# Pacing the modulation products by weight tiles, a third buffer for their weight, and silu of c by exp and ln

## The chip, the cores and the metric

The kernel runs on one core of a Trainium2 chip. The metric is device time in microseconds (us) for one execution of the whole program, and the median of several executions stands for a kernel. The engines are named as in the profile: PE is TensorE, DVE is VectorE, ACT is ScalarE, POOL is GpSimd, and SP is SyncE, which issues nearly all the DMAs here.

## The reference

Two blocks are chained on 256 tokens of width 1024. The first holds a mixed layer (mLSTM and a sparse attention, "NSA") and an HGRN2 layer. The second is modulated by a vector `c`:

```python
c_act = jax.nn.silu(c)
for i in range(DEPTH):                     # DEPTH = 2
    mod = c_act @ ada_w[i] + ada_b[i]      # (1, 1024) @ (1024, 6144)
    sh1, sc1, g1, sh2, sc2, g2 = jnp.split(mod, 6, axis=-1)
    h = modulate(rmsnorm(x, norm_mix_g[i]), sh1, sc1)
    y = pool_mixer(h, ...) if i == 0 else sgu_mixer(h, ...)
    x = x + g1[:, None, :] * y
    h = modulate(rmsnorm(x, norm_mlp_g[i]), sh2, sc2)
    x = x + g2[:, None, :] * (jnp.square(jax.nn.relu(h @ mlp_w1[i])) @ mlp_w2[i])
return rmsnorm(x, final_g)
```

The modulation needs only `c` and `ada_w`, nothing of `x`. So its 2 x 48 products (128 columns each) may be done anywhere between the arrival of `c` and the first use of their result.

## The kernel before

**Weight tiles.** All large products go through 128x1024 weight pieces. `load_raw` (L142) fetches two pieces, 1 MB, into a buffer `raw` (three of them); `split_w` (L148) makes from each piece a rounded part `whi` on ScalarE (L153) and the rest `wlo` on VectorE (L154), four buffers each. `mm_T` (L207) then does 24 matmuls for a piece: weight high by activation high (L212), weight high by activation low (L213), weight low by activation high (L214). `tiles_tok` does the same with the roles swapped (L197 to L199). Results leave PSUM through VectorE (`nt`, L301).

**Stages in time.** The mixed layer takes 35 pieces of `ev_w_in` and 8 of `ev_w_out`, with the NSA and mLSTM steps (generators `ns` and `ml`) between them; the HGRN layer takes 32 pieces of `od_w_in` and 8 of `od_w_out`; then come the pool mixer, the first MLP (32 pieces of its first matrix, 32 of its second), the SGU mixer and the second MLP. In the profile these start at about 0, 197, 345, 382 (second matrix 478), 570 and 645 us.

**Modulation.** `ada` (L328) is a generator. Each of its 72 steps takes one or two of the 96 tiles: a DMA of 512 KB into a buffer `araw` (L341, two buffers), then one VectorE instruction that multiplies it by silu of c (`row_c`) and sums along the row into a column of `mod` (L342). Eight tiles are six steps. Silu of c is made after the first NSA and mLSTM steps: one tanh on ScalarE (`tanh(th, crow)`, shown at L371, the line of the table helper) and two VectorE instructions (L489, L490); the scratch is an `araw` buffer.

**What sets the order.** Code calls `step(upto)` at hand-chosen places. The tile scheduler then orders every engine's queue by priority and by free buffers; a step stands there with its priority moved (`tc.high_priority(offset=-50)`). The engines execute their queues in order, so a VectorE instruction that waits for its DMA holds up everything behind it, the `wlo` of the next weight piece among it, and SP's DMA issues wait in the same way for a free buffer.

Of the kernel before, what the change touches and what calls it, by code (L numbers as in the profile page):

```python
# [65 lines left out]
def tile_kernel(ctx: ExitStack, tc: tile.TileContext, io: dict, out: bass.AP):  # L66
# [115 lines left out]
    def tile_T(ps, w, i, pair):  # L182

        wh, wl = w.piece(i, 128)
        mm_T(ps, lambda k: wh[:, k, :], lambda k: wl[:, k, :], pair.hi, pair.lo, range(KT))

    def tiles_tok(w, i, pair, evict):

        ps = [gbank()[:, :256] for _ in range(2)]
        for half in range(2):  # L190
            wh, wl = w.piece(i + half, 256)
            for tb in range(2):
                ts_ = slice(tb * 128, tb * 128 + 128)
                for k4 in range(4):
                    k = half * 4 + k4
                    st, sp = k == 0, k == KT - 1
                    PE.matmul(ps[tb], pair.hi(k)[:, ts_], wh[:, k4, :], start=st, stop=False)  # L197
                    PE.matmul(ps[tb], pair.lo(k)[:, ts_], wh[:, k4, :], start=False, stop=False)  # L198
                    PE.matmul(ps[tb], pair.hi(k)[:, ts_], wl[:, k4, :], start=False, stop=sp)  # L199
        for tb in range(2):  # L200
            evict(tb, ps[tb])
# [102 lines left out]
    def out_proj(src, pair, evict, side=0, every=1):  # L304
        w = Weights(lambda c: src[c])
        for n in range(8):
            if every and n % every == 0:
                step(side)
            ps = gbank()[:, :T]
            tile_T(ps, w, n, pair)  # L310
            evict(n, ps)
# [17 lines left out]
    def ada(crow):  # L329
# [5 lines left out]
        for layer in range(2):  # L335
            mod, gains = mods[layer]
            for i in range(6):
                for n in ((0, 1), (2,), (3,), (4, 5), (6,), (7,)):
                    for c in (i * 8 + j for j in n):
                        raw = mk(wpool, [128, 1024], F32, "araw", bufs=2)  # L340
                        nc.sync.dma_start(raw, io["ada_w"][layer, c])  # L341
                        V.tensor_tensor_reduce(raw, raw, crow, 1.0, P("ada_b", layer * 48 + c), ALU.mult, ALU.add, mod[:, c : c + 1])  # L342
# [6 lines left out]
    done = [0]  # L349

    def step(upto):

        if done[0] < 6 * upto:
            done[0] += 1
            with tc.high_priority(offset=-50):
                next(side[0])

    def finish(upto):
        while done[0] < 6 * upto:
            step(upto)  # L360
# [21 lines left out]
    def even_layer(norm, nxt, w):  # L382
        with ExitStack() as es:
# [81 lines left out]
            def run(it, n=1):  # L465
                for _ in range(n):
                    next(it)
                    if early:
                        step(2)
# [3 lines left out]
            early = []  # L473
# [4 lines left out]
            row_sv = bcast_rows(ev, "sv")  # L478
            crow = bcast_rows(base, "c")
            columns(EV_TILES[4:11])  # L480
# [5 lines left out]

            th = mk(wpool, [128, 1024], F32, "araw", bufs=2)
            tanh(th, crow, scale=0.5)
            V.scalar_tensor_tensor(crow, th, 1.0, crow, op0=ALU.add, op1=ALU.mult)  # L489
            V.tensor_scalar(crow, crow, 0.5, None, op0=ALU.mult)  # L490
            side.append(ada(crow))
# [3 lines left out]
            early.append(1)  # L495
# [5 lines left out]
            early.clear()  # L501
# [8 lines left out]
            out_proj(io["ev_w_out"], y, add_x(nxt), 5, 2)  # L510
# [266 lines left out]
    def hgrn_layer(norm, nxt):  # L777
        with ExitStack() as es:
# [30 lines left out]
            def col(part, h, fn):  # L809
                ps = gbank()[:, :T]  # L810
                if part == 3 or h < 4:
                    step(5)
# [20 lines left out]
            def iv_cols(h0):  # L833
                for c0 in (h0 * 128, h0 * 128 + 256):
                    step(5)
# [109 lines left out]
            out_proj(io["od_w_out"], y, add_x(nxt), 5, 1)  # L945
# [46 lines left out]
    def mlp(layer, mod, norm, nxt):  # L992
        with ExitStack() as es:
# [6 lines left out]
            for n in range(32):  # L1000
                if layer == 0 and n % 2 == 0:
                    step(11)
                if layer and n % 4 == 3:
                    step(12)
# [11 lines left out]
            for n in range(8):  # L1016
                ps = gbank()[:, :T]
                for c in range(4):
                    if layer == 0 and c % 2 == 0:
                        step(11)  # L1020
# [31 lines left out]
    def sgu_layer(consts, mod, gains, norm, nxt):  # L1052
        with ExitStack() as es:
# [7 lines left out]
            def gelu_tile(dst, n):  # L1061
                step(11)
# [261 lines left out]
```

## Time and profile before

| | us |
|---|---|
| median of 3 executions | 840.6 |
| lowest, highest | 839.73, 841.76 |
| the profiled execution, its time | 842.29 |
| its span in the trace | 840.5 |
| PE busy in that span | 810.0 |
| DVE busy | 667.1 |
| ACT busy | 516.3 |

The profiled execution is 1.7 us above the median and 1.8 us longer than its own span. A matmul of a dense row of pieces is listed with about 283 ns, but these overlap: 24 of them follow each other within some 2.9 us. A busy PE is therefore told by the gaps that remain, which the profile lists with what ended them. A row of a window gives its start and end, its length, the busy time (and the count of instructions) of PE, PEld (TensorE's weight load), DVE, ACT and POOL, the granted TensorE clock as a share of full speed, the busy share of the DMA engines, and GB/s; a window asked for TensorE alone has its time only.

### The profile page before, as it was taken

How to read it: one execution, taken by the hardware profiler on the slowest of the kernel's cores; microseconds unless marked ns; L12 is line 12 of the kernel's file. 1: busy time of each engine (PE TensorE's matmuls, PEld its weight loads, DVE VectorE, ACT ScalarE, POOL GpSimd, SP SyncE). 2: the span in 40 equal slices, each digit the busy share in tenths (PEclk: the TensorE clock that was granted, in tenths of full speed). 3: DMA queues.
4: the chain of work that ended last, by engine and by line, in shares of the span. 5: the costliest groups of instructions: out<-in, count | busy, mean ns of one | idle time of the engine just before them, and what ended most of it. 6: DMA issues, size and time to landing. Idle time of an engine off the chain costs nothing.

```text
span 840.5 us, 17614 instructions
## 1 busy us (share of the span) xinstructions
PE 810.0 (96%) x7172; PEld 772.0 (92%) x7172; DVE 667.1 (79%) x1247; ACT 516.3 (61%) x918; POOL 4.9 (1%) x19
## 2 busy tenths in 40 slices
PE   6999999998999999999999998999999999999996
PEld 5989787888998998999999998999999999999995
DVE  7679888899999999999998977756678777754542
ACT  6645656686876565658777633445647777754431
POOL 0000000001000000000000000000000000000000
PEclk9999999999999999999999999999999999999998
DMA  9664266657785777667888888865445454554521
GB/s 328 220 221 171 101 198 218 233 180 265 293 310 201 239 254 282 228 226 246 310 277 289 297 298 295 296 208 194 152 151 185 166 198 161 193 188 168 196 102 50
DMA packets 34497, 184.72 MB, mean 220 GB/s; under 512 B 3825, under 2 KB 4465, under 8 KB 19057
## 3 DMA queue, kind: packets, MB, share of 16 engines
q1 hardware_dynamic: 33984, 182.85, 62.3%
q8 instruction: 56, 0.92, 0.4%
q10 hardware_dynamic: 432, 0.76, 0.3%
q14 instruction: 25, 0.20, 0.1%
HBM read 182.55 MB, written 1.05 MB: 218 GB/s over the span
## 4 chain that ended last, share of the span: by engine, by line
PE 66%; DMA 13%; DVE 10%; ACT 5%; issue 4%; SPq 0%; DVEq 0%; ACTq 0%
PE g L212 17%; PE g L214 17%; PE g L213 16%; DMA araw<-in_ada_w_dram 12%; DVE wlo L154 4%; DVE araw L342 3%; ACT whi L153 1%; PE m L848 1%; PE g L197 1%; PE g L198 1%; PE g L199 1%; PE m L739 1%; PE long L767 1%; PE m L285 1%; DVE nt L301 1%
## 5 line engine op out<-in xcount | busy, mean ns | idle before, releaser
L212 PE MATMUL g<-ahi,whi 128*128 128x258 f32 (+1 forms) x1256 | 359.6, 289 | 10.9 <-ACT whi L153 6.7
L214 PE MATMUL g<-ahi,wlo 128*128 128x258 f32 (+1 forms) x1256 | 356.6, 285 | 3.1 <-DVE wlo L154 3.1
L213 PE MATMUL g<-alo,whi 128*128 128x258 f32 (+1 forms) x1256 | 357.7, 286 | 0.1
L153 ACT CAST whi<-raw 128x1024 fp32r<-128x1024 f32 (+1 forms) x238 | 246.6, 1043 | 168.2 <-PE g L213 134.1
L154 DVE TENSOR_TENSOR wlo<-raw,whi 128x1024 fp32r<-128x1024 f32 (+1 forms) x238 | 289.2, 1217 | 73.7 <-ACT whi L153 73.2
L212 PEld LDWEIGHTS g<-ahi,whi 128*128 128x128 f32 x1256 | 238.3, 190 | 15.6 <-ACT whi L153 6.9
L214 PEld LDWEIGHTS g<-ahi,wlo 128*128 128x128 f32 x1256 | 238.9, 190 | 5.3 <-DVE wlo L154 4.3
L213 PEld LDWEIGHTS g<-alo,whi 128*128 128x128 f32 x1256 | 239.5, 191 | 2.6 <-issue 1.2
L214 PE MATMUL g<-ghi,wlo 128*128 128x256 f32 x512 | 144.5, 282 | 4.5 <-DVE wlo L154 4.4
L213 PE MATMUL g<-glo,whi 128*128 128x256 f32 x512 | 144.7, 283 | 0.0
L212 PE MATMUL g<-ghi,whi 128*128 128x256 f32 x512 | 144.7, 283 | 0.0
L342 DVE CUSTOM_DVE_ANT_0 araw<-araw,row_c,prm 128x1024 f32<-128x1024 f32 x96 | 122.6, 1280 | 25.8 <-DMA araw<-in_ada_w_dram 25.6
L214 PEld LDWEIGHTS g<-ghi,wlo 128*128 128x128 f32 x512 | 96.9, 189 | 5.8 <-DVE wlo L154 5.8
L213 PEld LDWEIGHTS g<-glo,whi 128*128 128x128 f32 x512 | 96.4, 188 | 0.1
L212 PEld LDWEIGHTS g<-ghi,whi 128*128 128x128 f32 x512 | 96.0, 187 | 0.0
L301 DVE TENSOR_TENSOR nt<-g,nrstd 128x256 f32<-128x256 f32 x133 | 55.6, 420 | 21.7 <-PE g L214 21.6
L1012 ACT ACTIVATE nt<-nt,nb 128x256 f32<-128x256 f32 x64 | 32.3, 507 | 19.5 <-DVE nb L1011 19.5
L271 ACT ACTIVATE ahi<-xT,gains 128x256 fp32r<-128x256 f32 x32 | 16.2, 506 | 38.7 <-DVE xT L321 38.0
L197 PE MATMUL g<-whi,ahi 128*128 128x256 f32 x112 | 32.7, 292 | 0.0
L198 PE MATMUL g<-whi,alo 128*128 128x256 f32 x112 | 32.0, 286 | 0.0
L199 PE MATMUL g<-wlo,ahi 128*128 128x256 f32 x112 | 32.0, 286 | 0.0
L277 ACT ACTIVATE sq<-xT 128x256 f32<-128x256 f32 x56 | 22.5, 404 | 12.0 <-DVE xT L321 10.9
(288 smaller groups left out, 824.8 us busy)
## 6 DMA issues: line engine op xcount, KB each, us to landing
raw<-in_mlp_w_dram SPq DMA_DIRECT2D x64, 1024.0 KB, 4.9
araw<-in_ada_w_dram SPq DMA_DIRECT2D x96, 512.0 KB, 5.1
raw<-in_ev_w_in_dram SPq DMA_DIRECT2D x17, 1024.0 KB, 5.4
raw<-in_od_w_in_dram SPq DMA_DIRECT2D x16, 1024.0 KB, 5.6
raw<-in_sgu_w_in_dram SPq DMA_DIRECT2D x8, 1024.0 KB, 4.7
raw<-in_ev_w_out_dram SPq DMA_DIRECT2D x4, 1024.0 KB, 4.9
raw<-in_od_w_out_dram SPq DMA_DIRECT2D x4, 1024.0 KB, 6.0
raw<-in_sgu_w_out_dram SPq DMA_DIRECT2D x4, 1024.0 KB, 4.8
```

Of the source, the lines that this page charges most:

```text
L153: S.copy(hi[:, c], r[:, c])
L154: V.tensor_sub(lo[:, c], r[:, c], hi[:, c])
L197: PE.matmul(ps[tb], pair.hi(k)[:, ts_], wh[:, k4, :], start=st, stop=False)
L198: PE.matmul(ps[tb], pair.lo(k)[:, ts_], wh[:, k4, :], start=False, stop=False)
L199: PE.matmul(ps[tb], pair.hi(k)[:, ts_], wl[:, k4, :], start=False, stop=sp)
L212: PE.matmul(ps, wh(k), ah(k), start=st, stop=False)
L213: PE.matmul(ps, wh(k), al(k), start=False, stop=False)
L214: PE.matmul(ps, wl(k), ah(k), start=False, stop=sp)
L277: S.activation(sq, xT[:, k, :], AF.Square)
L301: V.tensor_tensor(t, ps[:, :T], self.r, op=ALU.mult)
L342: V.tensor_tensor_reduce(raw, raw, crow, 1.0, P("ada_b", layer * 48 + c), ALU.mult, ALU.add, mod[:, c : c + 1])
L1012: S.activation(r, r, AF.Relu, bias=b)
```

## The change

- `step` loses its argument and its guard. All calls at hand-chosen places go away (the mixed layer, both output projections, the HGRN columns, both MLPs, the SGU), and the flag `early` with them.
- A counter of multiplied weight takes their place: `pace(8)` in `tile_T` and in the second matrix of an MLP, `pace(16)` in `tiles_tok`. A table `PACE` of (count, steps) pairs says how many steps are to be done by then, linear in between. It asks for 14 steps by the end of `ev_w_in`, 16 by the end of `ev_w_out`, 25 and 30 by the ends of the HGRN layer's two, 36 about the end of the MLP's first matrix, 60 about the end of its second, 66 and 72 after that. The pool mixer's two pieces call no `pace`, while the table leaves room for 16 there, so from the MLP on each point comes two pieces late.
- `araw` gets three buffers instead of two.
- Silu of c is made as `c * exp(-ln(1 + exp(-c)))`, right after `c` is loaded: two VectorE instructions and three ScalarE ones, of functions that the table set loaded there already has. The steps may start at once.

```diff
     def tile_T(ps, w, i, pair):
+        pace(8)
     def tiles_tok(w, i, pair, evict):
+        pace(16)
-    def out_proj(src, pair, evict, side=0, every=1):
+    def out_proj(src, pair, evict):
-            if every and n % every == 0:
-                step(side)
-                        raw = mk(wpool, [128, 1024], F32, "araw", bufs=2)
+                        raw = mk(wpool, [128, 1024], F32, "araw", bufs=3)
-    done = [0]
-    def step(upto):
-        if done[0] < 6 * upto:
-            done[0] += 1
-            with tc.high_priority(offset=-50):
-                next(side[0])
+    done = [0, 0]
+    PACE = ((88, 0), (280, 14), (344, 16), (600, 25), (664, 30), (936, 36), (1192, 60), (1320, 66), (1384, 66), (1640, 72))
+    def step():
+        done[0] += 1
+        with tc.high_priority(offset=-50):
+            next(side[0])
+    def pace(tiles):
+        u = done[1]
+        done[1] += tiles
+        for (u0, s0), (u1, s1) in zip(PACE, PACE[1:]):
+            if u0 <= u < u1:
+                while done[0] * (u1 - u0) < s0 * (u1 - u0) + (s1 - s0) * (u - u0):
+                    step()
             crow = bcast_rows(base, "c")
+            zc = mk(wpool, [128, 1024], F32, "araw", bufs=3)
+            V.tensor_scalar(zc, crow, -80.0, None, op0=ALU.max)
+            tab[0].activation(zc, zc, AF.Exp, scale=-1.0)
+            tab[0].activation(zc, zc, AF.Ln, bias=1.0)
+            tab[0].activation(zc, zc, AF.Exp, scale=-1.0)
+            V.tensor_tensor(crow, crow, zc, op=ALU.mult)
+            side.append(ada(crow))
             tab[0] = Table(EXP_TANH, tab[0])
-            th = mk(wpool, [128, 1024], F32, "araw", bufs=2)
-            tanh(th, crow, scale=0.5)
-            V.scalar_tensor_tensor(crow, th, 1.0, crow, op0=ALU.add, op1=ALU.mult)
-            V.tensor_scalar(crow, crow, 0.5, None, op0=ALU.mult)
-            side.append(ada(crow))
```

What the scheduler makes of it is seen in the queues of the built programs, in three places. In these rows L342 is listed as ISA, a second row without sources goes with it, and a name's number tells its buffer's use.

The first place is ScalarE's queue some 23 us into the program, where the first weight pieces after the norm are split (`whi`) and results go to `nqk`. Before:

```order
L443 ACTIVATE nqk_165<-nt_271,prm_71 128x256
L153 CAST whi_323<-raw_321 128x1024
L443 ACTIVATE nqk_165<-nt_303,prm_71 128x256
L153 CAST whi_355<-raw_321 128x1024
L598 ACTIVATE A_617<-nqk_165 128x512
L153 CAST whi_389<-raw_387 128x1024
```

Now:

```order
L452 ACTIVATE nqk_165<-nt_271,prm_71 128x256
L380 ACTIVATE araw_320<-araw_320 128x1024
L153 CAST whi_329<-raw_327 128x1024
L452 ACTIVATE nqk_165<-nt_303,prm_71 128x256
L380 ACTIVATE araw_320<-araw_320 128x1024
L153 CAST whi_361<-raw_327 128x1024
L380 ACTIVATE araw_320<-araw_320 128x1024
L153 CAST whi_395<-raw_393 128x1024
```

The three activations of silu (L380) stand one ahead of each of three casts.

The second place is VectorE's queue in the mixed layer, at about 86 us: the first block of the NSA softmax (`nsmc`, `nEc`, `nmx`), the mLSTM's convolution (`qk`) and the weight split (`wlo`). Before:

```order
L722 TENSOR_REDUCE nsmc_934<-nEc_942 128x8
L154 TENSOR_TENSOR wlo_1113<-raw_1110,whi_1112 128x1024
L723 RECIPROCAL nsmc_934<-nsmc_934 128x8
L420 SCALAR_TENSOR_TENSOR qk_161<-mqk_1024,prm_71,qk_161 128x256
L724 TENSOR_TENSOR nsmc_934<-nsmc_934,gtok_693 128x4x2
L420 SCALAR_TENSOR_TENSOR qk_161<-mqk_1064,prm_71,qk_161 128x256
L725 TENSOR_TENSOR nEc_942<-nEc_942,nsmc_934 128x8x15
```

Now:

```order
L154 TENSOR_TENSOR wlo_1058<-raw_1055,whi_1057 128x1024
L728 TENSOR_REDUCE nsmc_948<-nEc_956 128x8
L429 SCALAR_TENSOR_TENSOR qk_161<-mqk_1044,prm_71,qk_161 128x256
L729 RECIPROCAL nsmc_948<-nsmc_948 128x8
L429 SCALAR_TENSOR_TENSOR qk_161<-mqk_1044,prm_71,qk_161 128x256
L730 TENSOR_TENSOR nsmc_948<-nsmc_948,gtok_699 128x4x2
L342 ISA araw_1008,mod_9_88<-araw_1008,row_c_318,prm_71 128x1024
L342 ISA mod_9_88 128x1
L731 TENSOR_TENSOR nEc_956<-nEc_956,nsmc_948 128x8x15
L429 SCALAR_TENSOR_TENSOR qk_161<-mqk_1044,prm_71,qk_161 128x256
L342 ISA araw_1011,mod_9_88<-araw_1011,row_c_318,prm_71 128x1024
```

The weight split has moved ahead of the softmax's sum, and modulation tiles stand between the softmax's instructions where there were none.

The third place is SP's queue of DMA issues in the second matrix of the first MLP, from its fourth fetch on; `raw` is 1 MB of the matrix, `araw` 512 KB of modulation weight. Before:

```order
L144 DMA raw_972_6313<-in_mlp_w2_dram 128x2048
L341 DMA araw_1049_6976<-in_ada_w_dram 128x1024
L144 DMA raw_979_6376<-in_mlp_w2_dram 128x2048
L341 DMA araw_1058_7046<-in_ada_w_dram 128x1024
L341 DMA araw_1059_7049<-in_ada_w_dram 128x1024
L144 DMA raw_986_6440<-in_mlp_w2_dram 128x2048
L341 DMA araw_1065_7110<-in_ada_w_dram 128x1024
```

Now:

```order
L144 DMA raw_957_6269<-in_mlp_w2_dram 128x2048
L341 DMA araw_1414_9317<-in_ada_w_dram 128x1024
L144 DMA raw_966_6338<-in_mlp_w2_dram 128x2048
L144 DMA raw_972_6399<-in_mlp_w2_dram 128x2048
L144 DMA raw_981_6468<-in_mlp_w2_dram 128x2048
```

The last modulation DMA stands ahead of the fifth of sixteen fetches; eleven fetches follow each other alone. Before, modulation DMAs went on up to the fifteenth.

## Rows read from the trace of the kernel before

**Rows 1.** The page: engines' busy time; the chain that ended last, by engine.

```profile
PE 810.0 (96%) x7172; PEld 772.0 (92%) x7172; DVE 667.1 (79%) x1247; ACT 516.3 (61%) x918; POOL 4.9 (1%) x19
...
PE 66%; DMA 13%; DVE 10%; ACT 5%; issue 4%; SPq 0%; DVEq 0%; ACTq 0%
```

**Rows 2.** Windows by stage: length, busy us (count) by engine, clock, DMA.

```profile
20.00:84.00 64.00, 61.85 (x523) 56.76 (x523) 49.85 (x98) 36.42 (x54) 0.53 (x1) 1.00 0.58 208
84.00:136.00 52.00, 49.97 (x340) 41.95 (x339) 44.01 (x108) 34.04 (x95) 0.60 (x6) 0.97 0.51 173
136.00:197.00 61.00, 58.56 (x418) 48.78 (x416) 55.77 (x130) 40.88 (x102) 0.00 (x0) 1.00 0.61 207
197.00:243.00 46.00, 44.89 (x423) 43.82 (x424) 43.38 (x77) 36.11 (x60) 2.71 (x2) 1.00 0.81 290
243.00:300.00 57.00, 54.73 (x1137) 51.93 (x1136) 55.66 (x101) 36.01 (x60) 0.00 (x0) 1.00 0.66 227
300.00:370.00 70.00, 69.86 (x532) 65.30 (x531) 65.78 (x121) 41.49 (x74) 0.00 (x0) 1.00 0.73 259
370.00:478.00 108.00, 107.96 (x874) 106.26 (x874) 101.92 (x209) 80.41 (x149) 0.00 (x0) 1.00 0.80 277
478.00:570.00 92.00, 87.47 (x715) 85.96 (x714) 66.04 (x90) 36.62 (x46) 0.00 (x0) 1.00 0.81 279
```

**Rows 3.** Waits by engine and line: us in total, times, longest.

```profile
PE g L214 <- DVE wlo L154: 7.5, 8, 2.4
DVE araw L342 <- DMA araw<-in_ada_w_dram: 25.6, 25, 2.4
```

**Rows 4.** The modulation instruction, ns min/median/max; its DMA to landing, us.

```profile
L342 DVE CUSTOM_DVE_ANT_0 araw<-araw,row_c,prm x96: 1233/1280/1291, 106.2 to 544.1; 128x1024 f32<-128x1024 f32 x96
...
DMA to landing us min/median/max: 3.4/5.1/9.2
```

**Rows 5.** VectorE's waits for modulation weight: 197:243, 243:300, 300:370, 370:478 us.

```profile
DVE araw L342 <- DMA araw<-in_ada_w_dram: 1.3, 2, 0.9
...
DVE araw L342 <- DMA araw<-in_ada_w_dram: 1.3, 2, 0.8
...
DVE araw L342 <- DMA araw<-in_ada_w_dram: 1.6, 2, 0.8
...
DVE araw L342 <- DMA araw<-in_ada_w_dram: 4.9, 6, 1.5
```

**Rows 6.** Timeline (start, us, instruction, [idle before]): ScalarE at 74 us, TensorE at 25.

```profile
74.15 1.05 ACT L371 ACTIVATE araw<-row_c 128x1024 f32<-128x1024 f32 x1
...
24.99 0.39 PE L212 MATMUL g<-ahi,whi 128*128 128x256 f32 x1 [0.26 <-ACT whi L153]
```

**Rows 7.** Timeline of VectorE, 78 to 82 us: the silu of c.

```profile
78.30 1.21 DVE L489 SCALAR_TENSOR_TENSOR row_c<-araw,row_c 128x1024 f32<-128x1024 f32 x1
...
81.49 0.67 DVE L490 TENSOR_SCALAR row_c<-row_c 128x1024 f32<-128x1024 f32 x1
```

**Rows 8.** TensorE near 88 us: timeline, and a window with its clock.

```profile
88.29 0.58 PE L214 MATMUL g<-ahi,wlo 128*128 128x256 f32 x1 [1.26 <-DVE wlo L154]
...
86.00:92.00 6.00, 4.74 (x25) 0.72 0.02 4
```

**Rows 9.** The chain of waits within 84 to 197 us, by line.

```profile
by line: PE g L214 11.3%; PE g L212 10.5%; PE g L213 10.3%; PE m L739 9.5%; PE long L767 9.4%; PE m L760 6.2%; ACT A L744 3.0%; ACT whi L153 2.9%; PE long L768 2.4%; issue 2.3%; PE m L569 2.2%; DVE wlo L154 2.0%; PE m L579 1.8%; PE m L548 1
```

**Rows 10.** Timeline of TensorE in the chunk levels of the HGRN layer.

```profile
249.76 0.76 PE L848 MATMUL m<-hq,hk 128*32 128x32 f32 x64 [0.89 <-DVE hk L897]
...
254.91 0.75 PE L848 MATMUL m<-hq,hk 128*32 128x32 f32 x64 [1.35 <-DVE hk L897]
```

**Rows 11.** Second matrix of the first MLP: VectorE, TensorE, a window.

```profile
506.11 1.28 DVE L342 CUSTOM_DVE_ANT_0 araw<-araw,row_c,prm 128x1024 f32<-128x1024 f32 x1 [2.35 <-DMA araw<-in_ada_w_dram]
...
508.60 0.39 PE L214 MATMUL g<-ghi,wlo 128*128 128x256 f32 x1 [2.37 <-DVE wlo L154]
...
485.00:490.00 5.00, 4.42 (x37) 4.21 (x37) 4.16 (x7) 1.29 (x3) 0.00 (x0) 1.00 0.94 337
```

More of the change, by code (lines that the diff above doesn't have):

```diff
@@ L348, in tile_kernel @@
     side = []
-    done = [0]
-    def step(upto):
-        if done[0] < 6 * upto:
-            done[0] += 1
-            with tc.high_priority(offset=-50):
-                next(side[0])
+    done = [0, 0]
[4 more added lines that the diff above has]
+            next(side[0])
     def finish(upto):
         while done[0] < 6 * upto:
-            step(upto)
+            step()
[5 more added lines that the diff above has]
+                while done[0] * (u1 - u0) < s0 * (u1 - u0) + (s1 - s0) * (u - u0):
+                    step()
     class Table:
@@ L467, in run @@
                     next(it)
-                    if early:
-                        step(2)
             nout = mk(ev, [128, 4, T], F32, "nout")
             mout = mk(ev, [128, 4, T], F32, "num")
-            early = []
             columns(EV_TILES[:4])
@@ L494, in even_layer @@
             columns(EV_TILES[17:23])
-            early.append(1)
             run(ns)
@@ L500, in even_layer @@
                 run(ns, n)
-            early.clear()
             columns(EV_TILES[25:31])
@@ L509, in even_layer @@
             columns(EV_TILES[31:])
-            out_proj(io["ev_w_out"], y, add_x(nxt), 5, 2)
+            out_proj(io["ev_w_out"], y, add_x(nxt))
     def mlstm(ev, et, qk, v, gsb, num, tanh):
@@ L810, in col @@
                 ps = gbank()[:, :T]
-                if part == 3 or h < 4:
-                    step(5)
                 tile_T(ps, w, part * 8 + h, pair)
@@ L834, in iv_cols @@
                 for c0 in (h0 * 128, h0 * 128 + 256):
-                    step(5)
                     tiles_tok(w, 8 + c0 // 128, pair, lambda tb, ps: V.scalar_tensor_tensor(
@@ L944, in hgrn_layer @@
             finish(2)
-            out_proj(io["od_w_out"], y, add_x(nxt), 5, 1)
+            out_proj(io["od_w_out"], y, add_x(nxt))
     def pool_layer(band, mod, norm, nxt):
@@ L1000, in mlp @@
             for n in range(32):
[L1001 to L1004, printed above, removed]
                 if layer == 0 and n == 16:
@@ L1018, in mlp @@
                 for c in range(4):
-                    if layer == 0 and c % 2 == 0:
-                        step(11)
+                    pace(8)
                     wh, wl = w2.piece(4 * n + c, 128)
@@ L1061, in gelu_tile @@
             def gelu_tile(dst, n):
-                step(11)
                 ps = gbank()[:, : norm.pair.w]
```

## The prediction

> **What bounds the kernel now.** I read the page first. TensorE is busy 96% of the span, and the chain that ended last is two thirds TensorE and 13% DMA [rows 1]: a change can win only where TensorE still has a gap, and lose only where it opens one. Next I read the windows by stage [rows 2]; length minus TensorE's busy time is the gap. From 20 to 84 us it is 2.2 us, 84 to 136 us 2.0, 136 to 197 us 2.4, 197 to 243 us 1.1, 243 to 300 us 2.3, 300 to 370 us 0.1, 370 to 478 us nothing, and 478 to 570 us, the first MLP's second matrix, 4.5. The same rows show VectorE's load: 44.0 of 52 us and 55.8 of 61 us in the mixed layer, over 94% from 197 to 370 us and in the MLP's first matrix, but only 66.0 of 92 us in its second. So the largest gap is where VectorE has least to do. The waits tell why [rows 3]: TensorE waits for `wlo`, while VectorE waits 25 times and 25.6 us for modulation weight. One case [rows 11]: VectorE stands 2.35 us for `araw`, then does the tile, then the `wlo` for which TensorE has stood 2.37 us. A modulation tile takes 1.28 us, its DMA 5.1 us in the median [rows 4], so two buffers turn over about once in 6.4 us, or 3.2 us a tile.
>
> **Where the tiles go.** The table asks for more steps in the second matrix. The queues of the built program say otherwise, and I follow them: the scheduler takes a tile as soon as a buffer is free, and a third buffer lets it take them earlier. I counted the tiles in VectorE's queue between instructions that I can also find in the trace of before:
>
> up to the first softmax block (84 us): 0 before, 4 now; from there to the second block (136 us): 9, 13; to the end of the NSA output (197 us): 13, 16; to the first level product of the HGRN layer (243 us): 10, 11; in the levels (to 300 us): 8, 8; to the pool output (370 us): 16, 18; to the end of the MLP's first matrix (478 us): 23, 24; after that: 17, 2.
>
> **The change part by part**, in us of TensorE's time:
>
> (a) *The new silu, +1.0.* Its three activations stand ahead of three weight casts at about 23 us. An activation of this size took 1.05 us [rows 6], with tanh; I take exp and ln alike. TensorE already waits 0.26 us for such a cast there [rows 6], so the first pushes it by its whole length; the other two have nearly 3 us of matmuls a piece as cover. Bounds: 0, if the casts before give slack, and 3.2, all three. The two VectorE instructions fall between 20 and 84 us, where VectorE has 14.2 us free [rows 2].
>
> (b) *The old silu, -0.5.* Two VectorE instructions, 1.21 and 0.67 us [rows 7], leave a busy place at 78 to 82 us. Little of it was on the path, since the gap of the whole stretch is 2.2 us. Bounds -1.9 and 0.
>
> (c) *Seven more tiles from 84 to 197 us, +2.0.* They cost 7 x 1.28 = 9.0 us of VectorE. It has 8.0 + 5.2 = 13.2 us free there [rows 2], partly idle that it can't use, because it waits for TensorE's or ScalarE's part of a softmax. The chain in this stretch is mostly TensorE [rows 9], so VectorE's extra work is covered until it falls behind. The upper bound is +9.0, nothing covered. The lower is -3.0: at 88 us TensorE stood 1.26 us for a `wlo`, and the granted clock over 86 to 92 us was 0.72, with part of it at the lower level of 1.2 GHz after that stand [rows 8]. That is 0.28 x 6 = 1.7 us more, and both would go if the `wlo`, which now precedes the softmax sum, comes in time. But the next `wlo` comes behind two tiles, 2.6 us, so a like stand can open there. I take a value nearer to the covered end because the chain is TensorE's.
>
> (d) *197 to 243 us, 0.* One more tile, +1.3; VectorE's 1.3 us of waits for modulation weight [rows 5] go with the third buffer. Bounds -1.1 and +1.3.
>
> (e) *The HGRN levels, 243 to 300 us, -1.3.* The same number of tiles. VectorE waits 1.3 us for weight [rows 5], and TensorE stands 0.89 and 1.35 us for the VectorE instruction behind [rows 10]. Bounds -2.2 and 0.
>
> (f) *300 to 370 us, +0.5.* Two more tiles, 2.6 us, less 1.6 us of waits [rows 5], with 4.2 us free [rows 2]. Bounds -0.1 and +2.6.
>
> (g) *First matrix of the MLP, 0.* One more tile, 1.3 us, against 4.9 us of waits that a third buffer shortens [rows 5]. TensorE has no gap there, so no gain is possible. Bounds 0 and +1.3.
>
> (h) *Second matrix, -4.3.* Fifteen tiles leave. Ten of VectorE's waits were here, and TensorE's gap of 4.5 us is behind them [rows 2, 11]. The two that remain have three buffers. Bounds -4.5 and -2.3, if half of the gap stays at the start.
>
> DMA load moves with the tiles. In the second matrix one 5 us window shows 337 GB/s at a share of 0.94 [rows 11]; 15 tiles less are 7.9 MB less there, and each earlier stage gets at most 2.1 MB more per some 50 us, on 173 to 290 GB/s [rows 2]. I cost that at nothing; the cover is the 19% or more of DMA time that is free, and if it failed the loss would be one wait of the kind in [rows 11]. The Trainium skill (DMA: Bandwidth & Descriptors, Specifications) states about 358 GB/s as the limit of a core's share of HBM. That speaks against the table as written, not against the queues as built: 32 tiles and 16 fetches in the second matrix would be 33.6 MB, by the page 94 us where the stage now takes 92, which would be +2. No run here shows that rate held over a stage; the 337 GB/s lie below it.
>
> Sum: 1.0 - 0.5 + 2.0 + 0 - 1.3 + 0.5 + 0 - 4.3 = -2.6 us. The profiled execution took 842.3 us, so 839.7 on its own scale; the median of the runs shown is 840.6, 1.7 below it, so I say **838.0 us**.
>
> **The rivals.**
>
> *A, the mixed layer fills up (slower).* VectorE falls behind from 84 to 197 us and all of the 9.0 us shows; (c) becomes +9.0, the sum +4.4, the time 845.0. For it: 99.8 + 9.0 = 108.8 of 113 us would be busy [rows 2], in a stretch where VectorE must also wait for others, and a stand of TensorE can lower its clock [rows 8]. Against it: the chain is TensorE's [rows 9], and in the levels VectorE is busy 55.7 of 57 us while TensorE's gap is 2.3 us. The change is slower once (c) passes +4.6.
>
> *B, the two cancel (no change).* (c) is near +4.6, so what the second matrix gives back the mixed layer takes: 840.6.
>
> *C, the third buffer frees more.* The stand at 88 us and its slow clock go (-3.0 in (c)), and the levels lose both of TensorE's stands (-2.2 in (e)): the sum is 1.0 - 0.5 - 3.0 - 2.2 + 0.5 - 4.3 = -8.5, the time 832.1. For it: the `wlo` has moved ahead. Against it: more tiles stand in the same place.
>
> *D, the change does what its table says.* Then 32 tiles come in the second matrix, 33.6 MB. At 337 GB/s [rows 11] that is 99.7 us, 7.7 more than now; at the stage's own 279 GB/s [rows 2] 120, 28 more: 848 to 869. Against it: the queue, with two tiles after the first matrix.
>
> **How the numbers follow.** Chances: the forecast 0.39, A 0.21, B 0.23, C 0.15, D 0.02. A measurement of this kernel can tell about 0.2%, 1.7 us, from no change. The forecast is mostly faster (0.35 of 0.39), C is faster; B gives 0.20 of no change and the rest on both sides; A and D are slower. That is 0.51 faster, 0.25 the same, 0.24 slower. The range runs from C's 832 to just past A's 845; all bounds at one end at once lie outside.
>
> **What would show it.** Right: VectorE's waits for modulation weight fall from 25.6 us to under 8; the second matrix takes 87 to 89 us with a TensorE gap under 1 us; the mixed layer's output ends 1 to 4 us later; TensorE's stands in the levels are gone or halved. Wrong: TensorE waits for `wlo` between 84 and 197 us by more than 5 us in total, with a lower granted clock (A); no stand and full clock at 88 us (C); modulation tiles spread over the second matrix (D); or waits for modulation weight that stay in spite of three buffers, which would break (d) to (g).

## The result and the profile after

| | before | after |
|---|---|---|
| median, us | 840.2 | 847.0 |
| lowest to highest, us | 837.7 to 841.8 | 846.4 to 848.2 |
| ratio to before, 95% interval | | 1.0086 [1.0058, 1.0113] |
| profiled execution, us; its span | 842.3; 840.5 | 848.2; 846.4 |
| mean granted clock of that execution | 0.995 | 0.986 |

The change makes the kernel 0.8% slower by the medians of four executions each; forecast was 838.0 us, and the range ended just past 845. The page of after, its busy times and the chain that ended last:

```profile
PE 813.2 (96%) x7172; PEld 776.5 (92%) x7172; DVE 666.5 (79%) x1247; ACT 521.0 (62%) x920; POOL 4.9 (1%) x19
...
PE 87%; DVE 7%; ACT 3%; DMA 2%; issue 1%; SPq 0%; DVEq 0%; ACTq 0%
```

DMA has fallen to 2% of the chain (13% before, [rows 1]), and VectorE's waits for modulation weight have nearly gone, as forecast: 25.6 us before [rows 3], now

```profile
DVE araw L342 <- DMA araw<-in_ada_w_dram: 3.4, 4, 1.8
```

Yet the end came later. The stages of [rows 2] again, each cut at the same VectorE instruction in both programs; the columns are those of [rows 2]. First before, then after:

```profile
20.00:84.50 64.50, 62.35 (x527) 57.26 (x527) 50.35 (x100) 36.42 (x54) 0.63 (x2) 1.00 0.58 206
84.50:135.80 51.30, 49.27 (x335) 41.27 (x334) 43.34 (x106) 34.04 (x95) 0.50 (x5) 0.97 0.52 175
135.80:196.40 60.60, 58.58 (x418) 48.95 (x417) 55.49 (x128) 40.76 (x101) 0.00 (x0) 1.00 0.60 206
196.40:243.30 46.90, 45.37 (x427) 44.12 (x426) 44.13 (x82) 36.53 (x60) 2.71 (x2) 1.00 0.81 290
243.30:300.20 56.90, 54.63 (x1136) 51.83 (x1135) 55.56 (x100) 35.91 (x60) 0.00 (x0) 1.00 0.66 225
300.20:370.30 70.10, 69.96 (x533) 65.37 (x533) 65.88 (x122) 41.59 (x74) 0.00 (x0) 1.00 0.74 261
370.30:478.10 107.80, 107.76 (x873) 106.08 (x872) 101.72 (x209) 80.21 (x149) 0.00 (x0) 1.00 0.80 277
478.10:570.00 91.90, 87.37 (x714) 85.86 (x713) 65.94 (x90) 36.52 (x46) 0.00 (x0) 1.00 0.81 279
```

```profile
20.00:84.10 64.10, 60.52 (x488) 54.34 (x486) 52.07 (x104) 37.31 (x55) 0.63 (x2) 0.97 0.62 229
84.10:143.90 59.80, 53.03 (x363) 46.20 (x364) 52.43 (x120) 35.22 (x96) 0.51 (x5) 0.94 0.64 215
143.90:205.30 61.40, 58.99 (x424) 49.63 (x423) 57.25 (x134) 40.84 (x101) 0.00 (x0) 1.00 0.62 212
205.30:256.80 51.50, 48.86 (x432) 47.70 (x433) 46.41 (x87) 38.37 (x63) 2.70 (x2) 0.93 0.83 292
256.80:311.40 54.60, 53.35 (x1125) 50.41 (x1124) 54.11 (x97) 33.86 (x56) 0.00 (x0) 1.00 0.67 225
311.40:382.20 70.80, 70.24 (x536) 65.58 (x536) 67.77 (x126) 42.09 (x75) 0.00 (x0) 1.00 0.76 267
382.20:485.50 103.30, 103.25 (x836) 101.65 (x836) 102.34 (x211) 81.15 (x149) 0.00 (x0) 1.00 0.84 298
485.50:575.80 90.30, 90.28 (x751) 90.02 (x751) 49.49 (x59) 37.83 (x46) 0.00 (x0) 1.00 0.54 190
```

From the first softmax to the end of the NSA output 121.2 us stand for 111.9 before, and the next stage takes 51.5 for 46.9: 13.9 us lost in two stages. From there to the end of the MLP 319.0 us stand for 326.7, so 7.7 us are won. TensorE's gap in the second matrix, 4.5 us before, is 0.02. The clock from the first softmax to the second reads 0.94 (0.97 before), and behind the NSA output 0.93 (1.00 before).

The marks hide a part. TensorE's order around them has changed: 39 matmuls fewer lie in the first stage and 34 more in the next two. At 0.12 us each (24 of them take some 2.9 us) that is 4 to 5 us of work moved behind the first mark, so at equal work the first stage, 0.4 us shorter by its marks, is some 4 us longer. At the end of the NSA output both programs have done the same work again, 1275 matmuls since 20 us and 1280 by the windows, and the changed kernel is there 8.9 us later. A good part of the first 4 us lies at the new silu: from 20 to 34 us TensorE does 82 matmuls for 107 before, 3.0 us of work, and its clock falls behind a stand:

```profile
28.00:30.00 2.00, 2.00 (x12) 2.00 (x11) 1.72 (x2) 2.00 (x3) 0.00 (x0) 0.50 0.01 4
30.00:32.00 2.00, 2.00 (x14) 2.00 (x13) 0.94 (x2) 1.62 (x3) 0.00 (x0) 0.66 0.70 197
```

Before, it was 1.00 there. Finer windows around the two later losses, of TensorE alone:

```profile
108.00:114.00 6.00, 3.08 (x20) 0.94 0.68 190
114.00:120.00 6.00, 6.00 (x44) 0.77 0.42 162
...
208.00:216.00 8.00, 6.77 (x34) 0.57 0.88 339
```

TensorE is idle for half of the first window, and runs in the next at 0.77 of its clock: part of it at the lower of its two levels, 1.2 instead of 2.4 GHz. Over 208 to 216 us the loss is 0.43 x 8 = 3.4 us. Ahead of these lie stands, as idle time of TensorE that ends with another engine's work is called here. TensorE's instructions in order of time (start, duration, instruction, in brackets the idle time before it and what ended it):

```profile
26.00 0.39 PE L214 MATMUL g<-ahi,whi 128*128 128x256 f32 x1 [1.68 <-ACT whi L153]
...
94.40 0.39 PE L216 MATMUL g<-ahi,wlo 128*128 128x256 f32 x1 [1.42 <-DVE wlo L154]
...
112.84 0.39 PE L216 MATMUL g<-ahi,wlo 128*128 128x256 f32 x1 [2.40 <-DVE wlo L154]
...
206.21 0.62 PE L214 MATMUL g<-ahi,whi 128*128 128x256 f32 x3 [1.84 <-ACT ahi L206]
...
209.52 0.58 PE L214 MATMUL g<-ahi,whi 128*128 128x256 f32 x1 [1.23 <-DVE xT L315]
```

Before, the longest stand near the first place was 1.26 us [rows 8]. VectorE's instructions ahead of the stand at 206 us show why it waits:

```profile
200.55 1.28 DVE L342 CUSTOM_DVE_ANT_0 araw<-araw,row_c,prm 128x1024 f32<-128x1024 f32 x1
...
202.35 1.28 DVE L342 CUSTOM_DVE_ANT_0 araw<-araw,row_c,prm 128x1024 f32<-128x1024 f32 x1
...
203.56 0.29 DVE L443 TENSOR_SCALAR w<-nt 128x256 f32<-128x256 f32 x1
203.76 0.42 DVE L447 TENSOR_TENSOR nout<-nout,nt 128x256 f32<-128x256 f32 x1
204.09 1.28 DVE L342 CUSTOM_DVE_ANT_0 araw<-araw,row_c,prm 128x1024 f32<-128x1024 f32 x1
...
205.30 0.42 DVE L448 TENSOR_TENSOR nout<-nout,w 128x256 f32<-128x256 f32 x1
205.64 1.28 DVE L342 CUSTOM_DVE_ANT_0 araw<-araw,row_c,prm 128x1024 f32<-128x1024 f32 x1
...
206.84 0.42 DVE L207 TENSOR_TENSOR alo<-nout,ahi 128x256 fp32r<-128x256 f32 x1
```

The last piece of `nout` passes through a chain of small steps, `w`, `nout`, its split into `ahi` and `alo`, and only then can TensorE project it. Four modulation tiles of 1.28 us stand between these steps. Before, there were two, at

```profile
192.75 1.28 DVE L342 CUSTOM_DVE_ANT_0 araw<-araw,row_c,prm 128x1024 f32<-128x1024 f32 x1
...
195.22 1.28 DVE L342 CUSTOM_DVE_ANT_0 araw<-araw,row_c,prm 128x1024 f32<-128x1024 f32 x1
```

and TensorE's stands there were 0.75 and 0.56 us, at full clock. With two tiles more, 2.6 us, the stands are 2.2 us longer (1.84, 0.48 and 1.23 us), and half clock follows. Over the whole stage VectorE has time left (57.25 us busy of 61.4), but from 200 to 207 us it is busy throughout, most of it with tiles, and so it delays what TensorE waits for. Ahead of 112.84 us it looks the same, with tiles at 105.81 and 107.81 us:

```profile
107.81 1.28 DVE L342 CUSTOM_DVE_ANT_0 araw<-araw,row_c,prm 128x1024 f32<-128x1024 f32 x1
...
109.41 0.42 DVE L303 TENSOR_TENSOR nt<-g,nrstd 128x256 f32<-128x256 f32 x1
...
110.14 0.75 DVE L747 TENSOR_REDUCE nmx<-m 128x2 f32<-128x256 f32 x2
...
111.57 1.22 DVE L154 TENSOR_TENSOR wlo<-raw,whi 128x1024 fp32r<-128x1024 f32 x1
```

The theory from this (theory 1): what a tile costs depends on where it stands. In a chain that TensorE waits for it makes TensorE stand, and behind some of these stands TensorE also runs at 1.2 GHz for a while. Rivals: the load as such, each tile's time on VectorE wherever it stands (2); the third buffer's bursts (3); the early silu (4); the fetches that hold up others on SyncE's queue (5).

### The profile page after: what moved, and what is told of

Read it like the earlier page. It is cut to its first block, busy times and chain, and to the rows that moved or that the text cites. A ratio compares the mean times of both kernels' runs of the same rounds, so it can differ in the third digit from the quotient of the medians.

```text
span 846.4 us, 17598 instructions
## 1 busy us (share of the span) xinstructions
PE 813.2 (96%) x7172; PEld 776.5 (92%) x7172; DVE 666.5 (79%) x1247; ACT 521.0 (62%) x920; POOL 4.9 (1%) x19
## 3 DMA queue, kind: packets, MB, share of 16 engines
q1 hardware_dynamic: 33984, 182.85, 61.4%
## 4 chain that ended last, share of the span: by engine, by line
PE 87%; DVE 7%; ACT 3%; DMA 2%; issue 1%; SPq 0%; DVEq 0%; ACTq 0%
PE g L214 24%; PE g L216 24%; PE g L215 24%; DVE wlo L154 2%; PE m L851 2%; PE long L773 1%; ACT whi L153 1%; DVE araw L342 1%; PE m L745 1%; PE g L201 1%; PE g L199 1%; PE g L200 1%; DMA xT<-in_xT_dram 1%; PE m L287 1%; PE m L766 1%
## 5 line engine op out<-in xcount | busy, mean ns | idle before, releaser
L214 PEld LDWEIGHTS g<-ahi,whi 128*128 128x128 f32 x1256 | 240.8, 193 | 19.7 <-ACT whi L153 9.1
L216 PEld LDWEIGHTS g<-ahi,wlo 128*128 128x128 f32 x1256 | 241.4, 192 | 7.8 <-DVE wlo L154 6.8
L215 PEld LDWEIGHTS g<-alo,whi 128*128 128x128 f32 x1256 | 242.2, 193 | 3.7 <-issue 2.0
L342 DVE CUSTOM_DVE_ANT_0 araw<-araw,row_c,prm 128x1024 f32<-128x1024 f32 x96 | 122.1, 1278 | 3.5 <-DMA araw<-in_ada_w_dram 3.4
L1014 DVE TENSOR_TENSOR glo<-nt,ghi 128x256 fp32r<-128x256 f32 x64 | 26.9, 423 | 2.5 <-ACT ghi L1013 0.2
```

The source lines that it names most:

```text
L214: PE.matmul(ps, wh(k), ah(k), start=st, stop=False)
L215: PE.matmul(ps, wh(k), al(k), start=False, stop=False)
L216: PE.matmul(ps, wl(k), ah(k), start=False, stop=sp)
L1014: V.tensor_sub(glo[:, n, :], r, ghi[:, n, :])
```

## Experiments: one part at a time

**The third buffer alone**, on the kernel before (the old silu's scratch, which lies in the same buffers, is changed alike):

```
-  raw = mk(wpool, [128, 1024], F32, "araw", bufs=2)
+  raw = mk(wpool, [128, 1024], F32, "araw", bufs=3)
```

> The kernel before with three buffers for the modulation weight and nothing else. Its VectorE queue takes 12 and 11 tiles in the two halves of the mixed layer (before 9 and 13, changed kernel 13 and 16); the queue around the first softmax is that of before, and at the end of the NSA output two tiles stand behind the last product where four stood among its instructions. Theory 1 (stands: what costs is a tile in a chain of small steps that TensorE waits for, and the half clock after such a stand): no new stand, one half-clock stretch before the end as in before, the gap of 4.5 us in the second matrix goes, so 836 us (835 to 838). Rival 2 (load: each tile more in the mixed layer costs its 1.3 us): one tile more, 837 to 838, not to be told apart here. Rival 3 (the third buffer itself, by tiles in bursts): 843 to 847.

839.4 us, 0.9994 [0.9972, 1.0017]: a miss for theory 1 as I had placed it. The MLP won what was expected (from the pool output to the end of the SGU layer 275.6 us for 281.9), but a stand opened that I had not looked for, in the mLSTM between the two softmaxes, with two tiles ahead of the small product (L574) that the step before it needs. TensorE, then a window around it:

```profile
130.12 0.70 PE L579 MATMUL m<-w,ones 128*128 128x256 f32 x2 [2.00 <-ACT w L577]
```

```profile
116.00:136.00 20.00, 16.22 (x72) 11.78 (x72) 14.72 (x36) 9.55 (x36) 0.00 (x0) 0.74 0.75 240
```

0.26 x 20 = 5.2 us of clock, where the kernel before lost 1.7 at 88 us. Not all of it follows the stand shown: the clock is 0.57 from 118 to 126 us already (3.4 us), behind a stand of 1.30 us at 117 us for the same step, again with a tile just ahead. Theory 1 gets its mechanism, at another place; the buffer as such (3) is no cost in the sum.

**The changed kernel with two buffers** (the same line reversed, and the silu's scratch with it):

> The changed kernel with two buffers. Up to the second softmax block its VectorE queue is the changed kernel's row for row (13 tiles); behind it there are 11 tiles for 16, and at the end of the NSA output two tiles among the last instructions for four. 13 tiles stay for the second matrix. Theory 1: the stands at 85 to 95 and 113 us and their half clock stay, those at 206 to 215 us (3.6 us of stands, 2.9 us of clock) go for the most part, and the second matrix gives back 2 to 3 us: 843 to 846. Rival 2 (load): five tiles less, 840 to 842. Rival 3 (third buffer): all of the loss goes, 838 to 841.

846.4 us, 1.0060 [1.0036, 1.0084]: just past the end of what was expected. The loss up to the second softmax stays (+6.2 us there, +8.1 with three buffers), and one stand of 2.25 us comes back in the second matrix. Rival 3 falls.

**The new silu alone**, on the kernel before (the six lines of the new silu at their new place, the old ones out):

> The kernel before with the silu by exp and ln at its new place, two buffers and the old steps: 3 tiles up to 84 us, then 9, 12, 9, 8, 16, 23, 16. Theory on the silu: a stand of 1.3 to 1.7 us at 26 us and half clock behind it, 2.8 us at the marker near 54 us: 841 to 844, if the tiles that go early take nothing off later. If the early silu is not on the path: 840 to 841.

837.1 us, 0.9976 [0.9956, 0.9995]: faster, a miss. The stand is there,

```profile
25.29 0.39 PE L212 MATMUL g<-ahi,whi 128*128 128x256 f32 x1 [1.70 <-ACT whi L153]
```

but no lower clock followed it in this execution. The first softmax comes at 81.6 us for 84.5, but with 35 matmuls fewer done by then (492 for 527 since 20 us), so that is no gain yet. The gain comes later: the clock from the first softmax to the second is 1.00 (0.97 before), and in the levels TensorE has no stand as long as 0.3 us, where it had 0.89 and 1.35 [rows 10]. Whether the old silu or the places of the tiles, which moved too, had cost this is not shown.

**The old silu in the changed kernel:**

```
-  zc = mk(wpool, [128, 1024], F32, "araw", bufs=3)
   ...
   tab[0] = Table(EXP_TANH, tab[0])
+  th = mk(wpool, [128, 1024], F32, "araw", bufs=3)
+  tanh(th, crow, scale=0.5)
   ...
+  side.append(ada(crow))
```

> The changed kernel with the silu as in before (tanh, behind the first step of the mLSTM); the tiles stand as in the changed kernel: 4 to 84 us, 13 and 17 in the two halves, four at the end of the NSA output. Theory 1: the stand of 1.68 us at 26 us and the half clock from 28 to 31 us (1.7 us) go, 2.8 us at the marker near 54 us, the other stands stay: 843 to 845. Rival 4 (the early silu shifts all that follows and is the whole loss): 839 to 841. If it is not on the path: 847.

849.5 us, 1.0107 [1.0075, 1.0138], slower still: a miss. The tiles did not stay as expected: four now stand among the ten instructions of the first softmax, and TensorE stands 4.02 us at 90.7 and 3.05 us at 94.5 us for `nEc`. So this kernel does not price the silu. With the run before it, where the new silu alone made the kernel faster, rival 4 falls as the whole loss; these stands fit theory 1.

## Experiments: VectorE's time or the fetches

Of the first 33 tiles VectorE multiplies only 16 of 1024 elements; their fetches stay whole:

```
+  m = 16 if layer * 48 + c < 33 else 1024
-  V.tensor_tensor_reduce(raw, raw, crow, ...)
+  V.tensor_tensor_reduce(raw[:, :m], raw[:, :m], crow[:, :m], ...)
```

> The changed kernel; the first 33 modulation tiles are multiplied over 16 of their 1024 elements only, so these columns are not the reference's; their fetches are whole. It takes VectorE's time for them away and leaves SyncE's queue and the DMA load. The shorter instruction moves places too: 9, 10 and 16 pieces, and fewer of them in the first softmax. Theory 1: no stand above 1.5 us from 90 to 210 us, the end of the NSA output at 193 to 197 us, 835 to 839. Rival 5 (the fetches, which hold up the weight behind them on SyncE's queue, make the stands): the loss stays, 844 to 848.

827.4 us, 0.9819 [0.9788, 0.9849]. The end of the NSA output comes at 189.4 us, and the clock is 1.00 throughout both halves:

```profile
84.90:128.70 43.80, 43.12 (x317) 36.98 (x316) 34.65 (x109) 32.07 (x92) 0.50 (x5) 1.00 0.61 217
128.70:189.40 60.70, 60.52 (x438) 50.83 (x439) 45.04 (x135) 43.92 (x106) 0.00 (x0) 1.00 0.66 226
```

All fetches are in place, so rival 5 can't be the main cause. That it lies 14 us below the kernel before, more than expected, says that the tiles cost there too. The reverse, with whole instructions on VectorE and 16 columns fetched:

```
-  nc.sync.dma_start(raw, io["ada_w"][layer, c])
+  nc.sync.dma_start(raw[:, :16] if e else raw, ...)      # e: the first 33 tiles
+  V.tensor_tensor_reduce(raw, crow if e else raw, crow, ...)
```

> The reverse: of the first 33 modulation tiles only 16 of 1024 columns are fetched, and VectorE's instruction is whole, on other data, so these columns are not the reference's. 8, 10 and 16 pieces; four stand among the last instructions of the NSA output, as in the changed kernel. Theory 1: the stands at the end of the NSA output stay (3 us or more in sum from 195 to 210 us, and half clock behind them), 841 to 846. Rival 5: all of the loss goes, with the fetches, 834 to 839.

842.0 us, 1.0010 [0.9988, 1.0032], as theory 1 has it: stands of 1.85 and 1.24 us at 202.7 and 206.1 us, as in the changed kernel, with 3.4 us of clock. The 5 us below the changed kernel are not split between the fetches and the three tiles that changed places, so the fetches may have a share of up to 5 us.

## Experiments: the two places

**The first place.** The table starts at the end of the mixed layer:

```
-  PACE = ((88, 0), (280, 14), (344, 16), (600, 25), ...
+  PACE = ((344, 0), (600, 25), ...
```

> The changed kernel with the table started at the end of the mixed layer. The first half of the mixed layer gets 8 tiles for 13, and none in the 60 rows behind the first softmax, where the changed kernel has 6; the second half and the end of the NSA output stay row for row. Theory 1: the stands of 1.42 and 2.40 us and one half-clock stretch (1.7 us) go, 5 to 6 us: 841 to 843. Rival 2 (load): five tiles, 6.4 us less but most of it covered, 844 to 846, with the half clock staying. Rival 3: no change, 847.

840.6 us, 1.0003 [0.9985, 1.0021]: 6.5 us below the changed kernel's 847.0. From the first softmax to the second 51.3 us stand for 59.8; 17 of the 363 matmuls there have moved behind the second. At the end of the NSA output the kernel is 6.1 us earlier (199.2 for 205.3). The stands of 1.42 and 2.40 us are gone, and that at the end of the NSA output stays (2.84 us).

**The second place.** The scheduler takes tiles as early as buffers allow, so the table can't hold them: with its start put off to the end of the mixed layer, 28 tiles still came before the end of the NSA output (33 in the changed kernel). A true dependence does: the bias that a tile adds is written behind the last product of the NSA output.

```
+  gate = mk(base, [128, 96], F32, "agate")
   ...
+  bias = gate[:, j : j + 1] if j >= 28 else P("ada_b", j)
-  V.tensor_tensor_reduce(raw, raw, crow, 1.0, P("ada_b", j), ...)
+  V.tensor_tensor_reduce(raw, raw, crow, 1.0, bias, ...)
   ...
   columns(EV_TILES[31:])
+  V.scalar_tensor_tensor(gate[:, 28:96], nout[:, 3, :68], 0.0, P("ada_b", 28, 68),
+      op0=ALU.mult, op1=ALU.add)
```

> The changed kernel with the tiles from the 29th on held back (by the bias column) until the last product of the NSA output. VectorE's queue is the changed kernel's up to there, but the four tiles among the last 14 instructions of that output now stand behind its last product; five tiles more stay for the second matrix and behind. Theory 1: the stands of 1.84, 0.48 and 1.23 us from 206 to 210 us fall to the 1.3 us in sum of before and the half clock behind them (3.4 us) goes, 5 to 6 us: 841 to 843. If the second place is no cause: 847. Load alone (five tiles elsewhere): 845 to 847.

840.8 us, 0.9992 [0.9975, 1.0009]: 6.2 us below the changed kernel. The first place keeps its stand, the second has lost it:

```profile
114.75 0.38 PE L216 MATMUL g<-ahi,wlo 128*128 128x256 f32 x1 [2.40 <-DVE wlo L154]
...
206.96 0.39 PE L215 MATMUL g<-alo,whi 128*128 128x256 f32 x1 [0.51 <-DVE alo L207]
208.49 0.38 PE L214 MATMUL g<-ahi,whi 128*128 128x256 f32 x1 [0.54 <-DVE xT L315]
```

**Both:**

> Both places undone: the table started at the end of the mixed layer, and the tiles from the 24th on held back as above; 5, 8, 11, 11, 8, 18, 24 and 12 pieces. Theory 1: the two gains add up, 6.5 + 5.5 below the changed kernel: 834 to 837. If new stands open in their place: 839 to 841.

835.6 us, 0.9939 [0.9910, 0.9967]: the gains add up within the noise, 11.4 us for 6.5 and 6.2, and the kernel is faster than before. The windows from the first softmax to the second, to the end of the NSA output and to the first level product:

```profile
81.80:133.70 51.90, 50.28 (x346) 43.66 (x347) 45.61 (x107) 33.45 (x93) 0.51 (x5) 0.93 0.57 193
133.70:195.00 61.30, 59.79 (x420) 50.31 (x420) 52.27 (x125) 43.15 (x104) 0.00 (x0) 0.97 0.56 189
195.00:243.70 48.70, 48.20 (x452) 47.15 (x452) 46.70 (x85) 38.24 (x63) 2.71 (x2) 1.00 0.83 290
```

Half clock has not gone altogether: 3.6 us in the first (behind a stand of 1.35 us for `nt` that the changed kernel has too), 1.8 us in the second.

## Experiments: how many tiles the mixed layer should take

**Eight early, none in the mixed layer** (table ((48, 0), (56, 6), (344, 6), ...), bias held from the ninth tile to the end of the output projection), and the same with the silu written behind the columns that it preceded (its table asks for the eight from count 88 to 96 in place of 48 to 56):

> The changed kernel with eight modulation tiles asked for early (up to 84 us) and the rest held back by a true dependence: from the ninth on, the bias column that a tile adds comes from a small tile that is written behind the last product of the mixed layer's output. So the VectorE queue has 9 pieces (with the silu's) up to 84 us, none from there to the end of the NSA output (29 in the changed kernel), 10 from there to the first level product, then 9, 18, 24 and 27. Theory 1 (tiles in chains of small steps make TensorE stand, and its clock falls behind some stands): between 84 and 205 us no stand above 1.5 us, no half clock behind 100 us, the end of the NSA output at 190 to 194 us (before 196.4, changed 205.3); mean granted clock 0.99 or more; 832 to 836. Rival 2 (load only, the clock falls by chance in any order): the clock stays at 0.987 to 0.989, 837 to 841. If 27 tiles are too many for the second matrix, its gap comes back, 2 to 4 us on either.

> The same with the early silu written behind the columns that it preceded, so that its activations come later on ScalarE. Theory on the silu (three activations ahead of a weight cast make TensorE stand 1.68 us at 26 us and the clock fall behind it, 1.7 us): stand at 26 us down to 0.3 to 0.8 us, no half clock at 28 us, 1.5 to 3 us below the kernel with the gate alone: 830 to 834. If the silu is not on the path: the same as that kernel.

836.4 us, 0.9926 [0.9899, 0.9953]. The mixed layer is clean as expected, but eight tiles before 84 us opened a stand of 2.54 us at 60.5 us, and the clock from 54 to 66 us is 0.72. The second, 835.9 us, 0.9936 [0.9912, 0.9960], tests nothing: the scheduler left the silu where it was, with a stand of 1.65 us at 25.1 us.

**All held back** (old silu, table from 344 on, bias held from the first tile), with three buffers, with two, and with the hold ended at the last product of the NSA output:

> The changed kernel with the silu as in before (tanh) and all 96 modulation tiles held back by the bias column until the mixed layer's output projection has ended: none up to there, 11 to the first level product, 12 in the HGRN levels (8 before), 19, 24 and 30. Theory 1: no stand above 1.5 us up to 205 us and no half clock; the end of the NSA output at 187 to 192 us (before 196.4), 3 to 5 us of that given back in the levels, where VectorE is full; granted clock 0.995 or more; 827 to 833. Rival 2 (load only): the tiles only move from one full place to another, 836 to 840. Rival 4 (the early silu's stand is worth nothing, its like opens elsewhere): the same as the kernel with the gate and the early silu, 836.

> The same with two buffers: 0, 0, 0, 10, 14, 17, 23, 32 tiles. If the third buffer is worth what the MLP showed (6 us less from the pool output to the end of the SGU layer with three buffers), 833 to 838, with TensorE waiting for wlo in the second matrix again; if it is worth nothing where the tiles are held back, the same as with three.

> The kernel with none in the mixed layer, and the hold ended one place earlier, at the last product of the NSA output: two tiles come between the last product and the split that TensorE waits for, two more in front of the additions to x. All else stays. It prices one chain. Theory 1: TensorE stands 1 to 2.6 us longer between 185 and 200 us, with 0 to 1.7 us of half clock behind it: 1 to 4 us above the kernel with none. Rival 2 (load): VectorE is idle there, so no change, or less by the tiles that leave the levels.

With three: 840.0 us, 0.9985 [0.9963, 1.0007], a miss. The NSA output ended at 190.6 us and the clock was 0.995, as expected; but the levels and the stage behind took 134.2 us for 127.0 and so gave back 7.2 us, not 3 to 5, 1.8 of it by the clock (0.97):

```profile
238.60:298.10 59.50, 53.91 (x1104) 49.87 (x1103) 57.77 (x104) 33.00 (x56) 0.00 (x0) 0.97 0.72 241
298.10:372.80 74.70, 74.54 (x565) 69.59 (x564) 72.67 (x133) 43.78 (x75) 0.00 (x0) 1.00 0.79 272
```

VectorE is busy 97% of both: there the load (2) comes nearest to a bound. With two buffers 857.5 us, 1.0176 [1.0139, 1.0213]: VectorE waits 34.3 us for weight, so the third buffer is worth 17 us where the tiles come late, far more than expected. With the earlier end 837.1 us, 0.9960 [0.9936, 0.9985]: two tiles in front of the split cost TensorE nothing, since it had other matmuls (longest stand there 0.44 us), and tiles left the full levels. Theory 1 had this wrong: a chain costs only where TensorE has run out of other work.

**Four early, then none in the mixed layer, held to the last product of the NSA output** (new silu):

> The changed kernel, four tiles asked for early and the rest held back to the last product of the NSA output: 5, 0, 0, 12, 9, 17, 24 and 30 pieces. Theory 1: no stand above 1.8 us up to 205 us except the one at 26 us, the end of the NSA output at 188 to 191 us, 1 to 3 us given back from there to the pool output, 829 to 834. If the levels are the bound, as with all tiles held back: 836 to 840.

833.5 us, 0.9904 [0.9874, 0.9934]: the best, below both kernels. From the first softmax, the two halves of the mixed layer and, last row, the second matrix:

```profile
80.90:131.20 50.30, 49.50 (x363) 43.69 (x363) 37.35 (x91) 34.66 (x93) 0.61 (x6) 0.97 0.41 142
131.20:191.80 60.60, 60.41 (x434) 50.63 (x434) 42.45 (x107) 44.11 (x108) 0.00 (x0) 1.00 0.21 74
...
469.10:559.00 89.90, 89.90 (x750) 89.85 (x749) 76.48 (x110) 38.03 (x46) 0.00 (x0) 1.00 0.91 338
```

## Why the prediction was wrong

By its own terms, from the two profiled executions (us):

| term | forecast, bounds | measured | from |
|---|---|---|---|
| (a)+(b) silu, to 84 us | +0.5, -1.9 to +3.2 | -0.4 | 64.1 for 64.5, with 39 matmuls fewer: some +4 at equal work |
| (c) 84 to 197 us | +2.0, -3.0 to +9.0 | +9.3 | 121.2 for 111.9, with 34 matmuls more: some +5 at equal work |
| (d) 197 to 243 us | 0, -1.1 to +1.3 | +4.6 | 51.5 for 46.9, with 5 matmuls more: some +4 at equal work |
| (e) levels | -1.3, -2.2 to 0 | -2.3 | 54.6 for 56.9, with 11 matmuls fewer: some -1 at equal work |
| (f) to the pool output | +0.5, -0.1 to +2.6 | +0.7 | 70.8 for 70.1 |
| (g)+(h) first MLP | -4.3 | -6.1 | 193.6 for 199.7 |

The rest of the span differs by 0.1 us, and the sum is +5.9. What is given at equal work is an estimate, at 0.12 us a matmul.

**The step that failed is (c), and with it (d).** I priced the added tiles as VectorE time against free VectorE time, and took a value near the covered end "because the chain is TensorE's". What mattered was where they stand. The order had it: four tiles among the last instructions of the NSA output, where the trace before has two. I counted one tile more from 197 to 243 us and did not look at that row of the queue; (d) was left at 0 with bounds of one tile's length. In (c) I wrote that "a like stand can open there", and gave it no price; and the clock stood in the sum only as a possible gain, 1.7 us at 88 us, never as a loss. In place of +2.0 for (c) and 0 for (d) the runs show stands of 1.42 and 2.40 us in the one and of 1.84, 0.48 and 1.23 us in the other, with half clock behind some of them. The mixed layer's output came 8.9 us later, where 1 to 4 were forecast. The two places cost 11.4 us together by the medians. Without them the kernel is at 835.6 us; the forecast without (c) and (d), -4.6 us, would have been 836.0. That these agree is in part luck: (a) was too low and (g)+(h) not low enough.

**(a) was too low**, for the same missing term. Its stand came as forecast (1.68 us for 0.26 before, so +1.4 for +1.0), but the half clock behind it, 1.7 us (0.50 and 0.66 over 28 to 32 us), was priced at nothing; together they are about the 3.0 us of work that was missing at 34 us. No run undid it while all else stayed.

**How much of it is clock.** The mean granted clock, over the executions of each, is 0.996 before and 0.9875 after: 3 us and 11 us of the span. By that alone all of the 6.9 us between the medians could be clock. The undone places say otherwise. With the first undone the kernel is 6.5 us faster, and its mean clock over twelve executions is 0.988, no higher than the changed kernel's. With the second undone it is 0.991, some 3 of the 6.2 us. So nearly all that the first place cost in the mean was not clock, and about half of the second.

**Rival A** came nearest (845.0). Its sign was nearly met: TensorE waited 4.4 us for `wlo` between 84 and 206 us (2.0 before), not above 5, with a lower clock. Its reason, that VectorE is full, holds in the few us ahead of a stand, but not as a bound of the whole stretch. Each undone place took five tiles away, 6.4 us of VectorE's time, so the two gains by themselves fit load as well as place. What tells them apart is kernels with like numbers of tiles, one execution of each. The kernel before with the new silu does 24 tiles by the end of the NSA output and is there at 191.6 us; the one with the third buffer alone does 23 and is there at 199.8; the one with all held back does none, and comes at 190.6. So 24 tiles passed at a cost of 1 us, and 23 in other places at 9. The load told most in the levels, when tiles were held back into them.

**What held.** VectorE's waits for modulation weight fell below 8 us (3.4), the second matrix lost its gap, the levels won, no tiles spread over the second matrix. (g)+(h) was too small by 1.8 us: I took TensorE's gap as the whole gain, but its busy time held short waits too. The same 1587 matmuls were busy 195.1 us before and 193.5 after, both at full clock. (a)+(b) stood at +0.5, and the new silu alone gave 2 us, about 0.24% [0.05, 0.44]; how much of that is the old silu's going and how much the tiles' new places is open.

**Open.** Why the same stand is followed by half clock in one execution and not in another; what makes up the first place's 6.5 us beyond its two stands (3.8 us), as the mean clock did not rise when it was undone; what share the fetches have; and the silu's own stand at 26 us, which no kernel here removed while keeping the new silu.

## What to carry to other kernels

Price an instruction that is moved by the place that it gets in the queue: print that place, find the chain that the tight engine waits for, and ask whether it has other work meanwhile; free time over a stage doesn't answer that. Add the clock behind a stand of TensorE as a cost with a chance. Where a scheduler fills every idle slot, a table of counts doesn't hold work back; a true dependence does.

## What the runs showed of the hardware

- Half clock behind a stand cost 1.7 us in the kernel before at 88 us (0.28 x 6) and 3.4 us in the changed kernel at 212 us (0.43 x 8), and stands below 1.5 us were followed by it. It is not sure: a stand of 1.26 us at 88 us was followed by a granted clock of 0.72 in the kernel before [rows 8], and the same stand by full clock in the kernel with a third buffer alone; so was one of 2.98 us at 116 us in the changed kernel with the old silu.
- Executions of one kernel differ with it: with the third buffer alone the fastest, 836.9 us, had a mean clock of 0.991, the slowest, 843.4 us, 0.984. That is 0.007 of the span, 5.9 us, so the clock can make most of the spread of 6.5 us. Between kernels it doesn't tell the time: the kernel before has a mean clock of 0.996 and takes 840.2 us, that with a third buffer alone 0.988 and 839.4.
- In the last kernel's second matrix DMA moved 338 GB/s over 90 us while TensorE had no gap; 27 of the tiles fall into it. That is 30.4 MB. Rival D's loss of 8 us or more was worked out for 33.6 MB at 337 GB/s, so this is near its case, not the case itself. The Trainium skill (DMA: Bandwidth & Descriptors, Specifications) gives about 358 GB/s as a core's limit of HBM; the prediction said that no run showed that rate held over a stage, and 338 GB/s come near it. For a shorter time the traces go above that limit: from 10 to 20 us the kernel before moved 424 GB/s.
